# A hybrid streaming layer on one core: the sample tile's attention beside the last two tiles, in other slots, and two changes of timing in the scheduler

## The chip, the cores and the metric

The kernel runs on one core of one Trainium2 chip. The metric is device time in microseconds of the whole kernel; lower is better. A core has five engines that run side by side: TensorE (PE in the profile, with its weight loads as PEld), VectorE (DVE), ScalarE (ACT), GpSimd (POOL) and SyncE (SP), which issues most DMA transfers. Products go from PE into banks of PSUM, and ACT or DVE empty these.

## The reference

One encoder layer on 17 tiles of 128 frames: 16 tiles are one prompt of 2048 frames, and the last is the sample tile (8 running streams with 16 new frames each). Two mixers run on the same projection of the frames:

```python
p = jnp.einsum('btd,de->bte', x, w_in)      # q, k, v, gate of retention; q, k, v of attention
# retention, 4 heads of 128, by chunks, with a state s carried along
scores = jnp.einsum('bnhd,bmhd->bhnm', q, k) * dmask
o = jnp.einsum('bhnm,bmhe->bnhe', scores, v) + jnp.einsum('bnhd,bhde->bnhe', q, s) * q_decay
s_new = g * s + jnp.einsum('bmhd,bmhe->bhde', k * k_decay, v)
# banded attention, 8 query heads of 64 on 2 key heads: a chunk of 64 frames reads itself and two chunks before
p = sink_softmax(einsum(q, k_band) * 64 ** -0.5, sinks)      # one learned sink in the denominator
o = einsum(p, v_band)
# then
x = layer_norm(ALPHA * x + mix @ w_out);  y = layer_norm(ALPHA * x + relu(x @ w_up) ** 2 @ w_down)
```

For the sample tile each of the eight streams has its own cached window of 128 keys and values (`cache_swa_k`, `cache_swa_v`) beside its 16 new ones, and its own retention state (`state_ret`), of which the new one is an output.

## The kernel before, in words

**Tiles and groups.** The 17 tiles go in three groups: prompt tiles 0 to 4, tiles 5 to 10, and the sample tile (number 16) with tiles 11 to 15. In the third group the sample tile has index 0. Each group runs through the stages `kv`, `qk` (or `sq`), `ret`, `out`, `mlp`; tile names in the profile carry group and stage, so `sw_2ret` is a bank taken in stage `ret` of the third group (counted from 0). Single-precision operands are split into a rounded high part and the rest, and each product is three matmuls (`mm3`). In the second and third group, many products are made by a scheme of seven products in place of eight, for which sums and differences of operand blocks are needed: of weights (made once, kept in DRAM as `kept`, `keptd`, `keptq`, `keptv`) and of frames (`sums_task`, which makes T1 to T4 in the `xT` slots).

**Memory slots.** On-chip memory is cut into slots by tag: 14 `xT`, 10 `w`, 4 `raw`, 20 rows `y` of 512 numbers, 8 `u3` of 768, and in PSUM 2 banks `mm`, 2 `rt` and 4 `sw`. `take` takes a slot, `drop` gives it back, `room(tag, n)` asks whether n are free. `S.fence[name]` is the time, by the scheduler's own reckoning, when the last user of a slot is through with it.

**The scheduler.** The order of the instructions on each engine is fixed when the kernel is built, by a small scheduler (`Sched`). The main thread of the program issues the large products one after another; everything else is written as tasks (generators) that `yield` the time at which they want to go on. Before each three matmuls the main thread calls `S.pump()`, which lets the tasks run whose time has come by the scheduler's cost model. A `yield` thus puts off the issue of an instruction; what an engine does on the chip is then in that order. `S.ready(t, eng)` gives the reckoned time when t is written.

**What the change touches.**

- `sums_task` (stage `kv` and `qk`) makes T2 and T1, and when these are through, T3 and T4 in `xT` slots. In the third group, T1 and T2 are first stored to DRAM (`keptt`) since they are read again later. Its helper `put` copies the high part on ACT (L297), and makes the rest on DVE (L313).
- `vg_operands` makes 32 block sums of the gate and value weights during the MLP of the second group, each on a DVE and ACT pass, and stores them as `keptv`. `due` spaces them.
- `swa_task` goes through the attention of the five prompt tiles of the third group, in the order of indices 3, 4, 5, 1, 2. For the scores of a tile it takes all four `sw` banks; its softmax runs on DVE (row maximum, L337) and ACT (exponentials, L293).
- `swa_sample_task` does the sample tile's attention in two halves of four streams. It loads cached keys and values, makes scores (PE, 64x144), exponentials, transposes and value products. Before the change it starts when `swa_task` has ended (`after[3]`), and its buffers are `u3` slots.
- `pair_task` does retention for one tile and two heads. For the sample tile, it loads the old states of each head (`sold`), masks the values by stream (`vm`), makes the outputs, and in two `sw` banks the new states (`kvs`).
- `vg_units` is the main thread in stage `ret` of the third group: seven products times three pairs of tiles of the gate and value projection. Its `post` tasks empty the banks and start the retention of a tile when its parts are there.
- `units` is the order of the output projection, as pairs of half and tile index. In the loop over it, the next unit is staged (`stage_mix`, which waits until retention and attention of that tile are issued) before the products of the present one are issued:

```python
S.until(lambda: u in mts and all((h, units[ui + 1][1]) in ret_tasks for h in range(RH)))
stage_mix(units[ui + 1])
```

Of the kernel before, what the change touches and what calls it, by code (L numbers as in the profile page):

```python
# [14 lines left out]
P = 128  # L15
# [38 lines left out]
VGT = (2,)  # L54
# [125 lines left out]
def tile_layer(ctx: ExitStack, tc: tile.TileContext, A: dict, O: dict):  # L180
# [17 lines left out]
    def room(tag, n=1):  # L198
        return live[tag] + n <= CAP[tag]
# [5 lines left out]
    def take(tag, shape, dt=F32):  # L205
        if not room(tag):
            assert not S.inside, f"no room in {tag}"
            S.until(lambda: room(tag))
        live[tag] += 1
        cnt[0] += 1  # L210
        t = (psp if tag in PS else sb).tile(shape, dt, tag=tag, bufs=CAP[tag], name=f"{tag}_{ph[0]}_{cnt[0]}")
        name = t.tensor.name if hasattr(t, "tensor") else t.name
        tag_of[name] = tag
        S.fence[name] = min(freed[tag])
        freed[tag].remove(S.fence[name])
        return t
# [32 lines left out]
    def wait_room(tag, n=1):  # L249
        while not room(tag, n):  # L250
            yield S.now + 0.3
# [456 lines left out]
    def vg_operands():  # L708

        while at_pair[0] < 1.0 or ph[0] != "1mlp":  # L710
            yield S.now + 1.0
        stored = []

        def save(kt, i, o, hl):
            yield S.ready(hl, eng="SP") - 0.3
            dma(kept_v[o][kt].rearrange("p (x c) -> p x c", x=2)[:, :, 256 * i:256 * i + 256],
                hl.bitcast(F32).rearrange("p (x c) -> p x c", x=2))
            drop(hl)

        due = 0.0  # L720
        for n_ in range(8):
            kt, i = n_ // 2, n_ % 2
            while not room("y", 3):
                yield S.now + 0.3
            src = [take("y", [P, 2, 256]) for _ in range(2)]
            for x in range(4):
                g_ = 4 * (x % 2) + kt
                o = 512 * (g_ % 2) + 256
                dma(src[x // 2][:, x % 2, :], A["wret"][2 * (x // 2) + i, g_ // 2][:, o:o + 256])
            yield S.ready(*src) + 1.5  # L730
            a11, a12, a21, a22 = [src[x // 2][:, x % 2, :] for x in range(4)]
            for o, t, args in (("S1", a22, (a21, a22, ALU.add)), ("S3", a21, (a11, a21, ALU.subtract)),
                               ("S2", a11, (a22, a11, ALU.subtract)), ("S4", a12, (a12, a11, ALU.subtract))):
                while not room("y") or S.now < due:
                    yield S.now + 0.3
                due = S.now + 6.0
                hl = take("y", [P, 512], F32R)
                yield max(S.ready(*src, eng="DVE"), S.fence[hl.tensor.name])
                yield from idle("DVE", QUIET)
                vtt(t, *args)  # L740
                yield S.ready(t, eng="ACT")
                acopy(hl[:, 0:256], t)
                yield S.ready(hl[:, 0:256], eng="DVE")
                vtt(hl[:, 256:512], t, hl[:, 0:256].bitcast(F32), ALU.subtract)
                stored.append(S.add(save(kt, i, o, hl)))
            drop(*src)
        while not all(t[3] for t in stored):
            yield S.now + 0.3
        made_v.extend(kept_v)
# [360 lines left out]
    def sums_task(gi, T, used):  # L1110


        parts = []
        while (gi, "kv", 1) not in pieces:
            yield S.now + 0.3
        for i in range(2):
            while not room("u3", 4):
                yield S.now + 0.3
            parts.append([take("u3", [P, 2, 384]) for _ in range(4)])
            for t, (b, kk) in zip(parts[i], ((0, 0), (1, 0), (1, 1), (0, 1))):  # L1120
                dma(t, x_source(gi, b, 2 * kk + i))

        def put(o, t, i, slack):
            h, l = (x[:, 2 * i:2 * i + 2, :] for x in T[o])
            yield S.ready(t, eng="ACT")
            acopy(h, t)
            yield S.ready(h, eng="DVE")
            yield from idle(slack=slack)
            vtt(l, t, h.bitcast(F32), ALU.subtract)
            used[o] = i + 1  # L1130
            drop(t)

        def home(o):
            while not room("xT", 2):
                yield S.now + 0.3
            T[o] = (take("xT", [P, 4, 384], F32R), take("xT", [P, 4, 384], F32R))

        yield from home("T2")
        for x11, x12, x22, x21 in parts:
            yield S.ready(x11, x12, x22, x21, eng="DVE")  # L1140
            yield from idle(slack=XSLACK)
            vtt(x11, x12, x11, ALU.subtract)
            vtt(x12, x22, x12, ALU.subtract)
            vtt(x22, x22, x11, ALU.subtract)
            vtt(x21, x21, x22, ALU.subtract)
        for n_, o in ((2, "T2"), (0, "T1")):
            if o == "T1":
                yield from home(o)
            for i in range(2):
                yield from put(o, parts[i][n_], i, XSLACK)  # L1150
            if gi in VGT:
                stores[gi, o] = S.add(store_sum(o, T[o], list(norms)))
        for n_, o, before in ((1, "T3", "T2"), (3, "T4", "T1")):
            while used.get(before) != "over":
                yield S.now + 0.3
            yield from home(o)
            for i in range(2):
                yield from put(o, parts[i][n_], i, SLACK)
        if gi in VGT:
            return  # L1160
        while used.get("T3") != "over":
            yield S.now + 0.3
        while not room("xT", 2):
            yield S.now + 0.3
        xagain[gi, 1, 0] = 0
        h, l = xblocks[gi, 1, 0] = (take("xT", [P, 4, 384], F32R), take("xT", [P, 4, 384], F32R))
        for p in range(2):
            yield from wait_room("u3")
            r = take("u3", [P, 2, 384])
            dma(r, x_source(gi, 1, p))  # L1170
            yield S.ready(r, eng="ACT")
            split(h[:, 2 * p:2 * p + 2, :], l[:, 2 * p:2 * p + 2, :], r)
            drop(r)
            xagain[gi, 1, 0] = 2 * p + 2
# [273 lines left out]


    def swa_sample_task(ti, si, sq_tasks, qTs, kTall, vall, mix, after):  # L1450
        while not sq_tasks[ti] or not sq_tasks[ti][3] or not after[3]:
            yield S.now + 0.5
        qT = qTs[ti]
        for hb in range(2):
            yield from wait_room("u3", 5)
            kt, cv, vn = take("u3", [P, 4, 144]), take("u3", [P, 4, P]), take("u3", [32, 4, P])
            dma(kt[:, :, 0:128], A["ck"][4 * hb:4 * hb + 4].rearrange("b p k -> p b k"))
            dma(cv, A["cv"][4 * hb:4 * hb + 4].rearrange("b k f -> k b f"))
            ks = si * P + 64 * hb
# [4 lines left out]
                b = 4 * hb + i  # L1464
                dma(vn[0:16, i, :], vall[16 * b:16 * b + 16, si, :])
            yield S.soon(kt, cv, vn, qT)
            while not (room("sw", 2) and room("u3", 2)):
                yield S.now + 0.3
            ps, p = [take("sw", [P, 2, 144]) for pr in range(2)], [take("u3", [P, 2, 160]) for pr in range(2)]
            for i in range(4):  # L1470
                b = 4 * hb + i
                for g in range(2):
# [20 lines left out]
            for pr in range(2):  # L1493
                yield S.soon(p[pr])
                yield from wait_room("sw")
                pt = take("sw", [P, 4, P])
                for i in range(2):
                    transpose(pt[:, i, :], p[pr][:, i, 0:128])
                    transpose(pt[0:32, 2 + i, :], p[pr][:, i, 128:160])
                drop(p[pr])  # L1500
                yield from wait_room("u3")
                pts.append(take("u3", [P, 4, P]))
                acopy(pts[pr][:, 0:2, :], pt[:, 0:2, :])
                vcopy(pts[pr][0:32, 2:4, :], pt[0:32, 2:4, :])
                drop(pt)
# [15 lines left out]
                    b = 4 * hb + i  # L1521
                    copy(mix[gs, :, 16 * b:16 * b + 16], ov[gs, i, :].rearrange("p (j t) -> p j t", j=4))
            drop(ov)
            drop(kt, cv, vn)
        dropq[0](qT)
        swa_done.add(ti)

# [121 lines left out]
    def pair_task(t, h0, ps, qTs_, kTs_, done_qk, mix, made=None):  # L1649
# [41 lines left out]
        if smp:  # L1691
            for g, h in enumerate(hs2):
                op, k = bk[:, 2 + g, :], ks[g]
                while not (room("u3", 4) and room("sw", 2)):
                    yield S.now + 0.3
                hs = [slice(64 * hb, 64 * hb + 64) for hb in range(2)]
                sold = [take("u3", [P, 4, P]) for hb in range(2)]
                qp, vm = take("u3", [P, 2, 320]), take("u3", [P, 4, P])
                for hb in range(2):
                    dma(sold[hb], A["st"][h][:, 4 * hb:4 * hb + 4, :])  # L1700
                gzero(qp)
# [351 lines left out]
    for gi, tiles in enumerate(GROUPS):  # L2053
# [306 lines left out]
            rope = take("xT", [P, 6, P])  # L2360
            dma(rope[:, 0:n, :], A["rope"][goff:goff + n].rearrange("t p c -> p t c"))
        ret_tasks = {}
        units = [(0, ti) for ti in ((0, 3, 4, 5, 1, 2) if gi == 1 else (1,2,0,3,4,5) if gi in VGT else (0, 1, 2, 4, 3, 5))[:n]] + [(1, ti) for ti in ((4, 0, 2, 1, 3) if n == 5 else (0, 1, 2, 4, 3, 5))]

        keep = ("y", "y", "u3", "y", "u3") if n == 5 else None
        boxes, mts, xrs = {}, {}, {}
# [616 lines left out]
```

## Time and profile before

| | us |
|---|---|
| median of 3 runs | 2249.87 (2247.48 to 2254.01) |
| the profiled execution | 2248.2 |
| its span, first to last instruction | 2246.4 |
| PE busy in the span | 2223.6 |
| DVE / ACT busy | 1636.1 / 1021.0 |
| mean granted clock of TensorE | 0.997 |

Busy times of engines overlap. Matmuls are pipelined, so a busy PE is not PE at its peak. Rows of the profile show the line of a helper (L278 is every matmul, L284 every transpose, L297 every ACT copy, L313 every DVE tensor-tensor), so the tile names tell the steps apart. In rows of the timeline come start, duration, engine, line, operation, out<-in, shapes and count, and in brackets the idle time ahead of the row with what ended it. In rows of stretches come start and end, length, the busy time (and instructions) of PE, PEld, DVE, ACT and POOL, the granted clock as a share of full speed, the busy share of the DMA engines and GB/s. In rows of waits come who waited for whom, the total, how often, and the longest.

### The profile page before, as it was taken

Reading aid. Unit: us, or ns where it says so; the run is one execution under the profiler, and the core shown is the slowest. Engines: PE = TensorE matmul, PEld = TensorE weight load, DVE = VectorE, ACT = ScalarE, POOL = GpSimd, SP = SyncE. Lnnn points to the kernel's source line nnn. Section 1 sums busy time; section 2 is a strip of 40 time slices with the busy share of each in tenths; the row PEclk is TensorE's granted clock in tenths of the full one; section 3 lists DMA queues with packets and bytes.
Section 4 is the critical chain, followed back from the end, with each engine's and each line's share of the span. In section 5 each row is a group of like instructions: output and inputs, shape, how many; then the busy total and the mean of one; then the engine's idle time right before and its main releaser. Section 6 shows DMA issues by size and latency. Waiting matters only on the chain. (4 is left out here: it accounts for less than half of the span.)

```text
span 2246.4 us, 34610 instructions
## 1 busy us (share of the span) xinstructions
PE 2223.6 (99%) x12149; PEld 1971.3 (88%) x12149; DVE 1636.1 (73%) x3564; ACT 1021.0 (45%) x2407; POOL 96.3 (4%) x131
## 2 busy tenths in 40 slices
PE   9999999999999999999999999999999999999998
PEld 7788889999999988789999899899778999999987
DVE  6767689787877577787788877796775955555557
ACT  5534645555545555473344443366343732222222
POOL 0000000000000000000000000000010000000002
PEclk9999999999999999999999999999999999999999
DMA  7646758999989836767899998999555577777776
GB/s 262 212 169 212 282 196 306 322 328 336 319 320 349 282 127 221 265 242 249 289 345 341 342 324 289 333 344 348 208 185 191 171 256 252 248 259 255 251 255 182
DMA packets 228830, 598.91 MB, mean 267 GB/s; under 512 B 23216, under 2 KB 80304, under 8 KB 228656
## 3 DMA queue, kind: packets, MB, share of 16 engines
q1 hardware_dynamic: 223472, 587.26, 74.5%
q0 software_dynamic: 5184, 9.44, 2.5%
q8 instruction: 96, 1.57, 0.3%
q14 instruction: 78, 0.64, 0.1%
HBM read 401.25 MB, written 185.86 MB: 261 GB/s over the span
## 5 line engine op out<-in xcount | busy, mean ns | idle before, releaser
L278 PE MATMUL sw_1mlp<-xT_1out,w_1mlp 128*128 128x384 f32 x1152 | 209.5, 336 | 0.2 <-DMA w_1mlp<-kept 0.2
L278 PE MATMUL sw_2mlp<-xT_2out,w_2mlp 128*128 128x384 f32 x1152 | 209.0, 336 | 0.3 <-DVE kvln_2mlp L313 0.3
L278 PEld LDWEIGHTS sw_1mlp<-xT_1out,w_1mlp 128*128 128x128 f32 x1152 | 202.0, 188 | 4.9 <-DMA w_1mlp<-kept 1.2
L278 PEld LDWEIGHTS sw_2mlp<-xT_2out,w_2mlp 128*128 128x128 f32 x1152 | 202.1, 188 | 4.3 <-DVE kvln_2mlp L313 0.6
L278 PE MATMUL sw_0mlp<-xT_0out,w_0mlp 128*128 128x320 f32 x1188 | 179.1, 309 | 0.0
L278 PEld LDWEIGHTS sw_0mlp<-xT_0out,w_0mlp 128*128 128x128 f32 x1188 | 176.5, 188 | 2.2
L278 PE MATMUL rt_2mlp<-w_2mlp,u_2mlp 128*128 128x512 f32 (+1 forms) x522 | 127.1, 388 | 0.0
L278 PE MATMUL rt_1mlp<-w_1mlp,u_1mlp 128*128 128x512 f32 x516 | 126.8, 391 | 0.0
L278 PE MATMUL rt_0mlp<-w_0mlp,u_0mlp 128*128 128x512 f32 x492 | 121.1, 391 | 1.5 <-DVE u_0mlp L313 1.4
L278 PE MATMUL mm_2mlp<-w_2mlp,u_2mlp 128*128 128x512 f32 (+1 forms) x504 | 122.5, 388 | 0.0
L278 PE MATMUL mm_1mlp<-w_1mlp,u_1mlp 128*128 128x512 f32 x492 | 121.3, 391 | 0.0
L278 PEld LDWEIGHTS rt_2mlp<-w_2mlp,u_2mlp 128*128 128x128 f32 x522 | 96.9, 188 | 19.0
L278 PEld LDWEIGHTS rt_1mlp<-w_1mlp,u_1mlp 128*128 128x128 f32 x516 | 96.5, 188 | 19.2
L278 PE MATMUL mm_0mlp<-w_0mlp,u_0mlp 128*128 128x512 f32 x456 | 112.2, 393 | 0.0
L278 PEld LDWEIGHTS rt_0mlp<-w_0mlp,u_0mlp 128*128 128x128 f32 x492 | 92.0, 188 | 20.7 <-DVE u_0mlp L313 1.9
L278 PEld LDWEIGHTS mm_2mlp<-w_2mlp,u_2mlp 128*128 128x128 f32 x504 | 93.6, 188 | 18.4
L278 PEld LDWEIGHTS mm_1mlp<-w_1mlp,u_1mlp 128*128 128x128 f32 x492 | 92.0, 188 | 18.3
L278 PEld LDWEIGHTS mm_0mlp<-w_0mlp,u_0mlp 128*128 128x128 f32 x456 | 85.9, 190 | 17.3
L313 DVE TENSOR_TENSOR w_1mlp<-w_1mlp,w_1mlp 128x512 fp32r<-128x512 f32 x120 | 81.7, 687 | 12.7 <-ACT w_1mlp L297 11.6
L313 DVE TENSOR_TENSOR w_0mlp<-raw_0mlp,w_0mlp 128x512 fp32r<-128x512 f32 (+1 forms) x69 | 63.5, 922 | 34.7 <-ACT w_0mlp L297 18.8
L297 ACT CAST u_2mlp<-kvln_2mlp 128x384 fp32r<-128x384 f32 x51 | 26.2, 515 | 117.7 <-PE mm_2mlp L278 44.1
L297 ACT CAST w_1mlp<-w_1mlp 128x512 fp32r<-128x512 f32 x84 | 52.0, 619 | 57.7 <-PE sw_1mlp L278 49.0
(1019 smaller groups left out, 4813.4 us busy)
## 6 DMA issues: line engine op xcount, KB each, us to landing
w_1mlp<-kept SPq DMA_DIRECT2D x104, 512.0 KB, 5.5
w_2mlp<-kept SPq DMA_DIRECT2D x104, 512.0 KB, 4.0
w_2mlp<-keptd SPq DMA_DIRECT2D x98, 512.0 KB, 4.2
kept<-w_0mlp SPq DMA_DIRECT2D x96, 512.0 KB, 5.0
keptd<-w_1mlp SPq DMA_DIRECT2D x84, 512.0 KB, 4.5
keptq<-y_0mlp SPq DMA_DIRECT2D x72, 256.0 KB, 5.1
w_1qk<-keptq SPq DMA_DIRECT2D x34, 512.0 KB, 5.9
w_2qk<-keptq SPq DMA_DIRECT2D x34, 512.0 KB, 6.9
```

Source lines behind the costliest of these rows:

```text
L278: S.run("PE", lambda: nc.tensor.matmul(out, lhsT, rhs, start=start, stop=stop, skip_group_check=again), [out], [lhsT, rhs], cost)
L297: S.run("ACT", lambda: nc.scalar.copy(out, in_), [out], [in_], 0.06 + 0.83e-3 * size(out))
L313: S.run("DVE", lambda: nc.vector.tensor_tensor(out, a, b, op), [out], [a, b], dcost(out))
```

## The change

Five edits:

1. `vg_operands`: the sums are spaced by 8.0 in place of 6.0.
2. `put` in `sums_task` yields until the slot that it writes is free by the scheduler's reckoning, and not only until its source is there.
3. `swa_sample_task` starts when three tiles' attention is done. Per half, if an `xT` slot and six rows are free, it takes its keys and values in one `xT` slot (`wide`) and the rest in rows `y`; else it takes `u3` slots as before.
4. `pair_task` for the sample tile takes the old states and masked values in rows `y` if five are free.
5. `units` of the third group begins with indices 1, 0, 2 in place of 1, 2, 0.

```diff
@@ vg_operands
-                due = S.now + 6.0
+                due = S.now + 8.0
@@ sums_task, put
-            yield S.ready(t, eng="ACT")
+            yield max(S.ready(t, eng="ACT"), *[S.fence[x.tensor.name] for x in T[o]])
@@ swa_sample_task
-        while not sq_tasks[ti] or not sq_tasks[ti][3] or not after[3]:
+        while not sq_tasks[ti] or not sq_tasks[ti][3] or len(swa_done) < 3:
...
-            yield from wait_room("u3", 5)
-            kt, cv, vn = take("u3", [P, 4, 144]), take("u3", [P, 4, P]), take("u3", [32, 4, P])
+            while not room("u3", 5) and not (room("xT") and room("y", 6)):
+                yield S.now + 0.3
+            tag = "y" if room("xT") and room("y", 6) else "u3"
+            vn = take(tag, [32, 4, P])
+            if tag == "y":
+                wide = take("xT", [P, 1088])
+                kt, cv = wide[:, 0:576].rearrange("p (b k) -> p b k", b=4), wide[:, 576:1088].rearrange("p (b k) -> p b k", b=4)
+            else:
+                kt, cv = take("u3", [P, 4, 144]), take("u3", [P, 4, P])
...
-            while not (room("sw", 2) and room("u3", 2)):
+            while not (room("sw", 2) and room(tag, 2)):
...
-            ps, p = [take("sw", [P, 2, 144]) for pr in range(2)], [take("u3", [P, 2, 160]) for pr in range(2)]
+            ps, p = [take("sw", [P, 2, 144]) for pr in range(2)], [take(tag, [P, 2, 160]) for pr in range(2)]
...
-                yield from wait_room("u3")
-                pts.append(take("u3", [P, 4, P]))
+                yield from wait_room(tag)
+                pts.append(take(tag, [P, 4, P]))
...
-            drop(kt, cv, vn)
+            drop(vn, *([wide] if tag == "y" else [kt, cv]))
@@ pair_task, sample tile
-                while not (room("u3", 4) and room("sw", 2)):
+                while not (room("sw", 2) and (room("u3", 4) or (room("u3") and room("y", 5)))):
...
-                sold = [take("u3", [P, 4, P]) for hb in range(2)]
-                qp, vm = take("u3", [P, 2, 320]), take("u3", [P, 4, P])
+                tag = "y" if room("y", 5) else "u3"
+                sold = [take(tag, [P, 4, P]) for hb in range(2)]
+                qp, vm = take("u3", [P, 2, 320]), take(tag, [P, 4, P])
@@ units
-        units = [... (1,2,0,3,4,5) if gi in VGT ...
+        units = [... (1,0,2,3,4,5) if gi in VGT ...
```

More of the change, by code (lines that the diff above doesn't have):

```diff
@@ L2362, in tile_layer @@
         ret_tasks = {}
-        units = [(0, ti) for ti in ((0, 3, 4, 5, 1, 2) if gi == 1 else (1,2,0,3,4,5) if gi in VGT else (0, 1, 2, 4, 3, 5))[:n]] + [(1, ti) for ti in ((4, 0, 2, 1, 3) if n == 5 else (0, 1, 2, 4, 3, 5))]
+        units = [(0, ti) for ti in ((0, 3, 4, 5, 1, 2) if gi == 1 else (1,0,2,3,4,5) if gi in VGT else (0, 1, 2, 4, 3, 5))[:n]] + [(1, ti) for ti in ((4, 0, 2, 1, 3) if n == 5 else (0, 1, 2, 4, 3, 5))]
         keep = ("y", "y", "u3", "y", "u3") if n == 5 else None
```

## The prediction

> **What bounds the kernel now.** I read the page's first part, then stretches of the stage that the change touches, then what TensorE (PE) waited for in it.
>
> ```profile
> span 2246.4 us, 34610 instructions
> PE 2223.6 (99%) x12149; PEld 1971.3 (88%) x12149; DVE 1636.1 (73%) x3564; ACT 1021.0 (45%) x2407; POOL 96.3 (4%) x131
> ```
>
> The profiled execution took 2248.2 us: this span and 1.8 us around it. It lies 1.7 us under the median of the three runs, 2249.87 (2247.48 to 2254.01). PE is idle for 2246.4 - 2223.6 = 22.8 us in all, so no edit that leaves its work as it is can win much more than 1%. This change leaves every product in place, so I look for the idle time it can reach. The stretches below are the third group's gate and value products with three of its attention tiles (1569.2 to 1628.5), the same with the last two tiles (to 1669), with the sample tile (to 1686.5), the first output unit with the sample tile's rest (to 1702.9), and output units alone.
>
> ```profile
> core 0: us, PE busy (x) PEld busy (x) DVE busy (x) ACT busy (x) POOL busy (x), PEclk, DMA share, GB/s
> 1569.20:1628.50 59.30, 56.67 (x347) 42.87 (x345) 44.60 (x130) 22.18 (x77) 3.35 (x5) 0.97 0.60 211
> 1628.50:1669.00 40.50, 40.33 (x282) 31.04 (x278) 30.43 (x96) 17.87 (x66) 3.91 (x8) 1.00 0.58 195
> 1669.00:1686.50 17.50, 17.50 (x143) 15.22 (x142) 14.10 (x56) 8.26 (x33) 2.64 (x4) 1.00 0.43 149
> 1686.50:1702.90 16.40, 15.52 (x135) 13.10 (x133) 12.88 (x51) 7.28 (x26) 1.60 (x4) 1.00 0.49 174
> 1702.90:1740.80 37.90, 37.90 (x172) 31.13 (x169) 19.72 (x41) 12.04 (x27) 1.62 (x2) 1.00 0.59 205
> ```
>
> PE's idle time here is 2.63, 0.17, 0, 0.88 and 0 us: 3.7 us where the change works. PE's waits from 1566 to 1703 name it:
>
> ```profile
> PE sw_2ret L278 <- ACT u_2ret L293: 2.3, 1, 2.3
> PE rt_2out L278 <- ACT xT_2ret L293: 0.6, 1, 0.6
> PE rt_2ret L278 <- ACT y_2ret L293: 0.3, 1, 0.3
> PE rt_2ret L278 <- ACT xT_2ret L293: 0.3, 1, 0.3
> ```
>
> The long one stands in the timeline of PE at 1609.2, and the clock row by row shows that it costs more than its gap:
>
> ```profile
> 1608.14 1.09 PE L278 MATMUL rt_2ret<-u_2ret,u_2ret 128*64 128x128 f32 x16
> 1611.51 2.47 PE L278 MATMUL sw_2ret<-u_2ret,y_2ret 64*128 64x512 f32 x4 [2.27 <-ACT u_2ret L293]
> 1609.20:1611.50 2.30, 0.04 (x2) 0.00 (x0) 0.61 (x3) 1.58 (x7) 0.00 (x0) 1.00 0.68 218
> 1612.50:1613.50 1.00, 1.00 (x3) 0.10 (x1) 0.69 (x1) 1.00 (x7) 0.00 (x0) 0.63 0.00 0
> 1613.50:1614.50 1.00, 1.00 (x4) 0.59 (x3) 0.48 (x1) 0.55 (x4) 0.00 (x0) 0.50 0.27 104
> 1614.50:1615.50 1.00, 1.00 (x6) 1.00 (x6) 0.20 (x1) 0.00 (x0) 0.00 (x0) 0.50 0.42 158
> 1615.50:1616.50 1.00, 1.00 (x8) 1.00 (x7) 0.00 (x0) 0.00 (x0) 0.00 (x0) 0.67 0.70 262
> ```
>
> The clock lost there is 0.37 + 0.50 + 0.50 + 0.33 = 1.7 us of full-speed work, so this one wait is worth 2.3 + 1.7 = 4.0 us. [...]
>
> **The frame sums ask for their slot first (the max with S.fence in put).** At present the ACT copy is issued while its slot is still being stored to DRAM, and what stands behind it on ACT and DVE waits too:
>
> ```profile
> 1528.71 0.83 ACT L297 CAST xT_2qk<-u_2kv 128x768 fp32r<-128x768 f32 x1 [11.57 <-DMA keptt_T<-xT_2kv]
> 1530.66 0.96 DVE L313 TENSOR_TENSOR xT_2qk<-u_2kv,xT_2qk 128x768 fp32r<-128x768 f32 x1 [9.56 <-DMA keptt_T<-xT_2kv]
> 1529.97 4.43 PE L278 MATMUL mm_2qk<-xT_1mlp,w_2qk 128*128 128x384 f32 x24 [0.91 <-ACT y_2qk L297]
> 1534.29 1.83 DVE L313 TENSOR_TENSOR xT_2qk<-u_2kv,xT_2qk 128x768 fp32r<-128x768 f32 x2 [1.13 <-DMA keptt_T<-xT_2qk]
> 1542.56 2.76 PE L278 MATMUL rt_2qk<-xT_2qk,w_2qk 128*128 128x384 f32 x15
> ```
>
> ACT stood for 11.57 us with copies that empty PSUM queued behind it, and PE ran out of a bank for 0.91 us. The new wait is in the kernel's own scheduler, not on the engine, so the PSUM copies pass. I take -0.9. What is late next is the sum itself: its splits end at 1536.1 now and its first reader on PE starts at 1542.56, 6.4 us of cover. Without that cover each later us would be PE's. Bounds: -0.9 if the wait goes, and +0.6 (the largest of the short waits above) if the splits come late instead. The wait is the row itself, so I stay at that end.
>
> **Weight sums spaced wider (6.0 to 8.0).** These are the 32 block sums of the gate and value weights, made in the second group's MLP.
>
> ```profile
> L359 SPq DMA_DIRECT2D keptv_S<-y_1mlp x32: 524/525/1396, 1095.6 to 1321.8; - x32
> L359 SPq DMA_DIRECT2D w_2qk<-keptv_S x1: 332/332/332, 1567.4 to 1567.4; - x1
> 1096.00:1322.00 226.00, 225.82 (x1140) 204.64 (x1139) 183.23 (x342) 101.93 (x211) 0.00 (x0) 1.00 0.97 341
> ```
>
> 32 stores in 226.2 us are 7.3 us apart. With 2 us more for each of 31 steps the last would fall 62 us later, at 1384; with 8.0 us as the whole step it falls at 1344. The first reader is at 1567.4, so at least 183 us cover it. Two source rows and one result row are held up to 62 us longer. The DMA engines are at 0.97 of their time there and get a little easier, but PE is idle for only 0.18 us of that stretch: 0, with bounds -0.2 and +0.6 (again a short wait, should the longer hold of rows stop something).
>
> **The sample tile's retention in rows.** The old states and the masked values move from u3 slots to y rows when five rows are free. Its loads, memset, copies and products are the same in number, so it issues nothing more on SP or POOL. It asks for two sw banks as before; and the long wait above is just that: the state product (sw out of u3 and y) sits in a bank that a softmax of the third attention tile still reads on ACT. A place in y does not free that bank. I take 0. Bounds: -4.0 if the small shifts ahead of it put the two in another order, and +4.0 if they make a second such wait; 0 is nearest to the row, since the code that chose the bank is untouched.
>
> **The sample tile's attention after three tiles instead of after five.** Its place in PE's order now, with the output units behind it:
>
> ```profile
> 1626.85 1.68 PE L278 MATMUL rt_2ret<-u_2ret,kvln_2kv 128*64 128x256 f32 x16
> 1645.55 1.68 PE L278 MATMUL sw_2ret<-u_2ret,kvln_2kv 128*64 128x256 f32 x16
> 1665.62 1.68 PE L278 MATMUL sw_2ret<-u_2ret,kvln_2kv 128*64 128x256 f32 x16
> 1668.98 1.20 PE L278 MATMUL sw_2ret<-u_2ret,raw_2qk 64*64 64x144 f32 x16
> 1692.10 1.20 PE L278 MATMUL sw_2out<-u_2ret,raw_2qk 64*64 64x144 f32 x16
> 1701.71 1.30 PE L278 MATMUL sw_2out<-u_2out,u_2ret 128*64 128x64 f32 x32
> 1702.94 4.43 PE L278 MATMUL mm_2out<-w_2ret,u_2out 128*128 128x512 f32 x18
> 1686.50:1704.20 17.70, 3.53 (x56) 2.85 (x56) 1.56 (x4) 3.27 (x18) 1.00 0.45 162
> ```
>
> The first three rows are the value products of the third, fourth and fifth tile. The sample tile's scores follow the fifth at once, its second half at 1692.1, and its end at 1703.0; the second output unit starts on it. So the sample tile now spans 34.0 us. The last row, on the banks of the second half alone, prices a half: PE 3.53, DVE 1.56, ACT 3.27 us. All of that moves to after 1628.5, and none of it is removed. Moving 7.1 us of PE work out of a tail that holds 0.88 us of idle time wins at most 0.88. In the tail remain the retention tasks of the last tiles, whose chain through ACT and DVE made both waits there (0.6 and 0.3), now with 48 output products between them where 24 stood. Where the work goes, DVE has 30.43 of 40.5 us busy and gets at least 3.1 more (83%), ACT 17.87 and 6.5 (60%). That leaves both below full, but a short wait can come of it. The loads of cached keys and values go out earlier on SP; DMA is at 0.58 there. They hold one xT slot and three rows (six must be free at the start), which value products and thirds of retention also ask for. I take -0.9 for the tail and +0.4, the mean of the two waits at 0.6 and 0.3, for a new one: -0.5, with bounds -0.9 and +6 (below).
>
> **Output units in the order 1, 0, 2.** Same products. It makes the loop ask for the sample tile one unit sooner. 0 if that tile is done by 1686.5.
>
> **The sum.** 2248.2 - 0.9 + 0 + 0 - 0.5 = 2246.8 us; at the median's distance that would be 2248.5.
>
> **Rivals.**
> *The long wait goes too.* Everything ahead of 1609 shifts by the 0.9 us and by other slots; the state product needs to come only about 2.3 us later, or ahead of that tile's scores. For it: one coincidence of two tasks. Against it: the same check for the bank. 2246.8 - 4.0 = 2242.8. [...]
>
> *The sample tile comes too late (the slower one).* The loop stages the next unit before it issues the present one, so with the sample tile second, no output product leaves before that tile is done. Begun at 1628.5, its 34.0 us end at 1662.5, 24 us ahead of 1686.5. But each attention tile wants all four sw banks, and tiles come 18.7 and 20.1 us apart; if each half must wait for one such turn, that is 38.8 us, and the end is at 1701 again. Then 24 products (18 take 4.43, so 5.9 us) are lacking as filler, and gaps like the one at 1609 lose 1.7 us of clock: 2248.2 - 0.9 + 5.9 + 1.7 = 2254.9, or 2253.2 without the clock; 2254. It decides from an end later than 1686.5.
>
> *The change doesn't act:* rows and xT slot are not free at 1628.5, the task falls back to u3 or waits, and ACT still meets the unfinished store: 2248.2.
>
> *PE is not full.* Weight loads (PEld) are at 0.72, 0.77, 0.87 and 0.80 in the first four stretches against 0.821 among plain output units. At 0.821 all through, the 102.2 us of loads there would take 124.5 us in place of 133.7: 9.2 us less, 2248.2 - 9.2 - 0.9 = 2238.1. [...] Against it speaks the 1.68 us for the same 16 products in each of three places: small products are slow wherever they stand, and an order does not mend that.
>
> **How the numbers follow.** About 0.3% (6.7 us) is what a measurement of this kernel can tell from no change. Forecast 0.50 (own range 2244 to 2250); long wait gone 0.23; too late 0.14; no effect 0.08; PE not full 0.05. Faster by over 0.3% means below 2241.5: the last case and two fifths of the second, 0.05 + 0.09 = 0.14. Slower means above 2254.9: half of the late case and a little of the forecast for a second long wait, 0.07 + 0.03 = 0.10. The same: 0.76. The range goes down to 2240, past the 4.0 us, and up to 2254.
>
> **What would show it.** Right: no ACT wait of many us on keptt; no PE wait of mm_2qk on y_2qk; the last store from y_1mlp to keptv_S between 1344 and 1384; 64x144 scores soon after the third tile's value products and an end before 1686; the state product's wait on ACT near 1609 still there, with half clock behind it; less than 0.5 us idle between the last value product and the second output unit. Wrong: that wait gone, or a new PE wait above 1 us, first of all on the sample tile's result before the first output unit, or on a PSUM bank between 1628 and 1686.

## The result, and the profile after

| | before | after |
|---|---|---|
| median, same chip | 2249.87 us (2245.65 to 2254.01, 9 runs) | 2243.05 us (2240.72 to 2244.95, 9 runs) |
| ratio | | 0.9973, 95% interval 0.9963 to 0.9983 |
| profiled execution, its span | 2248.2, 2246.4 | 2241.8, 2240.0 |

The change wins 0.27%, about 6 us by the ratio; the medians differ by 6.8. The time lies in the predicted range, but 3.8 us under the forecast of 2246.8 and outside that forecast's own range (2244 to 2250). It is nearest to the rival "the long wait goes too" (2242.8), to which I gave a chance of 0.23. Both of these count from the profiled 2248.2: as a change, 1.4 us less was forecast and 5.4 less by that rival, and the profiled executions differ by 6.4.

The first row of after's page, and what PE waited for from the start of stage `qk` to the end of the output projection:

```profile
PE 2221.1 (99%) x12149; PEld 1969.8 (88%) x12149; DVE 1636.8 (73%) x3564; ACT 1021.9 (46%) x2407; POOL 95.8 (4%) x131
```

```profile
PE rt_2ret L278 <- DMA y_2ret<-in_st_dram: 0.6, 2, 0.5
PE rt_2ret L278 <- ACT xT_2ret L293: 0.3, 1, 0.3
PE sw_2ret L284 <- ACT u_2ret L293: 0.3, 1, 0.3
PE sw_2ret L278 <- DMA u_2ret<-in_ck_dram: 0.2, 1, 0.2
```

PE is idle for 2240.0 - 2221.1 = 18.9 us in all, where it was 22.8. The wait of 2.3 us is gone, that of `mm_2qk` too (before, it stood at 1529.97 with 0.91). What is left is short. The first, third and last row are new, and the first and last are waits for loads: of old retention states (`in_st`) and of cached keys (`in_ck`).

To see where the time came from I cut both traces at the first PE row of a stage; these are the rows of after, and the first products of `qk`, `ret` and `mlp` are where the cuts are:

```profile
1476.09 1.73 PE L278 MATMUL sw_2qk<-xT_1mlp,w_1mlp 128*128 128x384 f32 x9
1565.58 1.78 PE L278 MATMUL mm_2ret<-w_2qk,xT_1mlp 128*128 128x512 f32 x7
1760.87 0.60 PE L284 MATMUL sw_2mlp<-cst,y_2out 128*128 128x128 f32 x4
```

And of before:

```profile
1478.57 1.21 PE L278 MATMUL sw_2qk<-xT_1mlp,w_1mlp 128*128 128x384 f32 x6
1569.25 1.08 PE L278 MATMUL mm_2ret<-w_2qk,xT_1mlp 128*128 128x512 f32 x4
1767.58 0.60 PE L284 MATMUL sw_2mlp<-cst,y_2out 128*128 128x128 f32 x4
```

| stretch | before | after | difference |
|---|---|---|---|
| up to `qk` of the third group | 1478.57 | 1476.09 | -2.48 |
| `qk` | 90.68 | 89.49 | -1.19 |
| `ret` and output projection | 198.33 | 195.29 | -3.04 |
| the rest | 478.83 | 479.13 | +0.30 |

The first line is not shown to come from the change: PE has hardly a gap where the sums are made (0.04 us of 248, below), and in the profiled executions of the two kernels and the experiments that start lies anywhere from 1474.8 to 1480.2, with and without each edit. The two stretches in the middle hold 4.2 us of the 6.4 us between these two executions; that the time came so close to the rival's 2242.8 is in part luck, since 2.5 us stand in that first line.

In `qk`, the rows of PE and ACT of after at the place of the old wait, and the last split with its first reader:

```profile
1526.41 4.32 PE L278 MATMUL mm_2qk<-xT_1mlp,w_2qk 128*128 128x384 f32 x24
1526.61 0.48 ACT L297 COPY y_2qk<-sw_2qk 128x384 f32<-128x384 f32 x1 [1.60 <-PE sw_2qk L278]
1527.12 1.57 ACT L297 CAST xT_2qk<-u_2kv 128x768 fp32r<-128x768 f32 x2
1535.91 0.96 DVE L313 TENSOR_TENSOR xT_2qk<-u_2kv,xT_2qk 128x768 fp32r<-128x768 f32 x1 [0.16 <-ACT xT_2qk L297]
1538.89 4.32 PE L278 MATMUL rt_2qk<-xT_2qk,w_2qk 128*128 128x384 f32 x24
```

ACT's copies out of PSUM now pass ahead of the copy into the slot and wait there for nothing but PE; `mm_2qk` has no bracket. The price shows in the last two rows: the splits end at 1536.87, and the first product that reads them starts 2.0 us later, where there were 6.4 us.

In `ret`, the same banks before and after. Of before:

```profile
1601.12 1.13 PE L278 MATMUL sw_2ret<-u_2ret,y_2ret 64*128 64x512 f32 x4
1602.18 1.68 PE L278 MATMUL sw_2ret<-u_2ret,kvln_2kv 128*64 128x256 f32 x16
1604.91 1.57 PE L278 MATMUL sw_2ret<-kvln_2kv,raw_2qk 64*128 64x192 f32 x16
```

Of after:

```profile
1595.99 1.68 PE L278 MATMUL sw_2ret<-u_2ret,kvln_2kv 128*64 128x256 f32 x16
1599.04 1.13 PE L278 MATMUL sw_2ret<-y_2ret,y_2ret 64*128 64x512 f32 x4
1601.69 1.57 PE L278 MATMUL sw_2ret<-kvln_2kv,raw_2qk 64*128 64x192 f32 x16
1612.22 1.13 PE L278 MATMUL sw_2ret<-y_2ret,y_2ret 64*128 64x512 f32 x4
```

The 64x512 rows are the new states of the sample tile's heads, the 128x256 rows the second attention tile's values, the 64x192 rows the third tile's scores. Before, the order was head 0, values, scores, and PE came to head 1 at 1609.2, 4.3 us after the scores began, and waited 2.3 us until that tile's softmax left the bank. After, the values come first, then head 0, then the scores, and head 1 follows 10.5 us after them, at 1612.22; the softmax is over by then (its last row on ACT ends at 1609.54). Counted from the start of `ret`, the values come 2.5 us earlier than before, head 0 1.6 us later, the scores 0.5 us later, and head 1 6.7 us later than PE came to it before. A coincidence of two tasks is undone, though no edit says anything about their order.

The sample tile's attention of after (first half, second half, last products), and the tail:

```profile
1627.27 1.20 PE L278 MATMUL sw_2ret<-u_2ret,raw_2qk 64*64 64x144 f32 x16 [0.19 <-DMA u_2ret<-in_ck_dram]
1645.34 1.20 PE L278 MATMUL sw_2ret<-xT_2ret,raw_2qk 64*64 64x144 f32 x16
1662.31 0.68 PE L278 MATMUL sw_2ret<-y_2ret,y_2ret 32*64 32x64 f32 x16
```

```profile
1625.00:1664.00 39.00, 37.73 (x313) 28.61 (x312) 31.27 (x107) 19.41 (x90) 3.87 (x8) 1.00 0.58 186
1686.18:1702.90 16.72, 16.72 (x97) 14.40 (x96) 13.30 (x48) 5.70 (x15) 2.08 (x4) 1.00 0.52 174
```

It ends at 1663.0, 23 us ahead of the first output product. Only its second half is in the new slots; the first still took `u3`. The tail has lost its 0.88 us of idle time, but the stretch with the sample tile now holds 1.27 us.

### The profile page after: what moved, and what is told of

It is laid out like the page before. It is cut to its first block, busy times and chain, and to the rows that moved or that the text cites. A ratio compares the mean times of both kernels' runs of the same rounds, so it can differ in the third digit from the quotient of the medians.

```text
span 2240.0 us, 34600 instructions
## 1 busy us (share of the span) xinstructions
PE 2221.1 (99%) x12149; PEld 1969.8 (88%) x12149; DVE 1636.8 (73%) x3564; ACT 1021.9 (46%) x2407; POOL 95.8 (4%) x131
## 5 line engine op out<-in xcount | busy, mean ns | idle before, releaser
L313 DVE TENSOR_TENSOR w_1mlp<-w_1mlp,w_1mlp 128x512 fp32r<-128x512 f32 (+1 forms) x120 | 81.7, 686 | 14.9 <-ACT w_1mlp L297 14.0
L313 DVE TENSOR_TENSOR w_0mlp<-raw_0mlp,w_0mlp 128x512 fp32r<-128x512 f32 (+1 forms) x69 | 63.5, 921 | 34.8 <-ACT w_0mlp L297 18.9
```

The source lines that it names most:

```text
L313: S.run("DVE", lambda: nc.vector.tensor_tensor(out, a, b, op), [out], [a, b], dcost(out))
```

## The experiments

Theory A: edit 2 carries the gain, by the `qk` wait directly and by the order of states, values and scores in `ret`. Edit 3 pays nothing by itself. Theory B: moving the sample tile's attention carries it. Theory C: the retention rows (edit 4) moved the state product.

The kernels ran in three sessions, each beside the kernel before, whose medians there were 2247.9, 2249.93 and 2248.61 us. "Qk" and "ret, out" are the two middle stretches of the profiled execution, cut as above; "clock" is the granted clock of the whole span, averaged over the timed runs. The ratios are as recorded; they are not quotients of the medians and differ from those by up to 0.05%.

| label | edits | median us | ratio, 95% interval | qk | ret, out | head 1 waits | clock |
|---|---|---|---|---|---|---|---|
| (before, profiled) | none | | | 90.68 | 198.33 | 2.3 | 0.9977 (33 runs) |
| no_slot_first | 1, 3, 4, 5 | 2246.22 | 0.9995, 0.9986 to 1.0004 | 90.84 | 196.38 | 2.3 | 0.9975 |
| no_slot_first_later_head | the same, head 1 later | 2243.59 | 0.9983, 0.9974 to 0.9992 | 90.31 | 194.77 | none | 0.9985 |
| no_retention_rows | 1, 2, 3, 5 | 2242.55 | 0.9977, 0.9968 to 0.9986 | 89.50 | 197.20 | none | 0.9988 |
| spacing_alone | 1 | 2246.24 | 0.9994, 0.9985 to 1.0003 | 93.31 | 199.21 | 2.3 | 0.9978 |
| changed_again | all | 2242.55 | 0.9970, 0.9958 to 0.9982 | 89.50 | 196.15 | none | 0.9987 |
| two_edits | 2, 3 | 2244.60 | 0.9977, 0.9966 to 0.9988 | 89.49 | 196.12 | none | 0.9986 |
| attention_and_order | 3, 5 | 2251.42 | 1.0009, 0.9998 to 1.0019 | 90.97 | 201.04 | 2.3 | 0.9973 |
| early_loads | all, loads earlier | 2240.39 | 0.9957, 0.9941 to 0.9973 | 89.49 | 194.40 | none | 0.9988 |
| changed_beside_early | all | 2242.51 | 0.9976, 0.9967 to 0.9984 | 89.50 | 195.24 | none | 0.9987 |
| early_loads_again | all, loads earlier | 2240.26 | 0.9968, 0.9956 to 0.9980 | 89.49 | 193.75 | none | 0.9986 |
| attention_later_head | 3, head 1 later | 2244.84 | 0.9984, 0.9976 to 0.9993 | 91.16 | 194.37 | none | 0.9985 |

**Without edit 2.** The changed kernel, with the old line in `put`:

```diff
-            yield max(S.ready(t, eng="ACT"), *[S.fence[x.tensor.name] for x in T[o]])
+            yield S.ready(t, eng="ACT")
```

> The changed kernel without its second edit (put asks for its source alone again, as before); the four other edits stay. Theory A, that the second edit carries the gain, by itself (0.9 us on PE in qk) and by shifting the sample tile's retention against the third attention tile (4.0 us): ACT waits over 10 us on keptt again, PE waits about 2.3 us near 1609 with half clock behind it, and the time is that of the kernel before, 2248 to 2251 us. Theory B, that the sample tile's attention beside the last two tiles carries it: 2243 to 2246 us.

The gain is gone: the interval of the ratio holds 1. The median is 1.8 us under theory A's 2248 to 2251, in a session in which the kernel before was 2.0 us lower than in the first measurement. The profile has all three old waits, on ACT, in `qk` and at head 1, though four of the five edits are in; the half clock that I expected behind the last one did not come (1.00 from 1610 to 1618, see the last section).

```profile
1526.59 0.83 ACT L297 CAST xT_2qk<-u_2kv 128x768 fp32r<-128x768 f32 x1 [11.74 <-DMA keptt_T<-xT_2kv]
1527.85 4.43 PE L278 MATMUL mm_2qk<-xT_1mlp,w_2qk 128*128 128x384 f32 x24 [1.08 <-ACT y_2qk L297]
1609.41 1.93 PE L278 MATMUL sw_2ret<-y_2ret,y_2ret 64*128 64x512 f32 x4 [2.27 <-ACT u_2ret L293]
```

The last row reads `y_2ret`: the old states lie in rows, and the wait is there all the same. So edit 4 does not take it away.

**The same, with head 1 later.** In `pair_task`, ahead of the second wait for banks:

```diff
                 yield S.soon(qp, vm, *sold)
+                if h == 1:
+                    yield S.now + 5.0
                 while not room("sw", 2):
```

> As the run without the second edit, and the sample tile's retention of head 1 puts off its last products by 5.0 us in the scheduler, so that the state product does not meet the banks of the third tile's softmax. It prices the long wait alone. Theory A: the wait near 1609 and its half clock go, the 11 us of ACT on keptt and 0.9 us of PE in qk stay: 3.5 to 4.5 us under the run without the second edit, about 2245. Theory B has the gain elsewhere: no change against that run beyond 1.5 us.

Head 1 then follows the scores by 10.0 us and does not wait (the row of its products stands at 1613.58 without a bracket). The median falls by 2.6 us against the kernel without these two lines: more than theory B's 1.5, less than the 3.5 to 4.5 of theory A. The `qk` wait is still there (0.5 us in this execution).

**Without edit 4.** The `pair_task` hunk of the diff undone.

> The changed kernel without its fourth edit: the sample tile's old states and masked values lie in u3 slots again. Theory A: the time of the changed kernel, 2242 to 2244 us; the two waits of PE on the loads of old states (0.6 us together in the changed kernel) may go. Theory C, that the other slots moved the state product away from the busy bank: the wait of 2.3 us near 1609 is back, about 2247.

The time of the changed kernel, and no wait at head 1: theory C falls for the state product. Its profile has two load waits, 1.8 and 1.2 us on `in_ck`, so its 197.20 is the longest stretch without the old wait; its profiled execution was also the slowest of its 11 runs (2247.80), so I read nothing further from it.

**Edit 1 alone.** `due = S.now + 8.0`, nothing else.

> The kernel before with the first edit alone (block sums of gate and value weights spaced by 8.0). Theory A: the last store moves from 1322 to 1344 to 1384 and nothing else, the time of before within 1 us. Theory D, that the DMA engines at 0.97 in that stretch cost something: 1 us or more faster.

No gain that can be told: the ratio stands for 1.3 us less, which would be theory D's side of 1 us, but the interval reaches from 3.4 us less to 0.7 us more. The last store is at 1355.3, as theory A has it. Its profile is of use for another reason: the two waits of before fell worse in it.

```profile
PE sw_2ret L278 <- ACT u_2ret L293: 2.3, 1, 2.3
PE mm_2qk L278 <- ACT y_2qk L297: 2.0, 1, 2.0
```

```profile
1530.00:1534.00 4.00, 4.00 (x16) 4.00 (x15) 2.17 (x3) 3.92 (x8) 0.00 (x0) 0.57 1.00 396
1612.00:1620.00 8.00, 7.46 (x22) 5.28 (x23) 2.99 (x12) 3.09 (x17) 0.46 (x1) 0.57 0.18 68
```

Behind the `qk` wait of 2.0 us the clock stood at 0.57 over 4 us, which is 1.7 us lost (4 x 0.43). Behind the wait at head 1 it stood at 0.57 over 8 us: 3.4 us lost.

**The changed kernel again**, and beside the kernels of the third session:

> The changed kernel as it is, beside the others on the same chip. All theories: 2242 to 2244.5, a ratio of 0.996 to 0.998 to the kernel before. Its profile shows again no wait on keptt, no wait of mm_2qk on y_2qk and no wait above 1 us of the sample tile's retention between 1600 and 1615.

> The changed kernel as it is, on the chip of the two others: 2241 to 2244.5, ratio 0.996 to 0.998 to the kernel before.

Both as expected: with the first measurement, ratios of 0.9973, 0.9970 and 0.9976, and `qk` 89.49 or 89.50 in each profile.

**Edits 2 and 3 alone.** Edit 2 was not measured by itself: with the old start of the sample tile's attention, the scheduler's tasks would wait for each other. So edit 3 goes with it, and what is said of edit 2 here holds with edit 3 in the kernel.

> Only edits 2 and 3: the frame sums ask for their slot, and the sample tile's attention starts after three tiles. Spacing, retention slots and unit order are as before. Theory A (edit 2 carries the gain, and needs edit 3 only so that the tasks don't wait for each other): the time of the changed kernel within 1.5 us, 2241.5 to 2245; no keptt wait, no mm_2qk wait, no 2.3 us wait on u_2ret. Theory C (retention in rows, or the order of the units, carries part of it): 1.5 to 4 us above the changed kernel.

A win of 0.23%, with the `qk` stretch of the changed kernel and the new order in `ret` (values 1599.11, head 0 1602.15, scores 1604.81, head 1 1615.58, no wait). Its median is 2.1 us above the changed kernel's, outside the 1.5 us of theory A and inside the range of theory C. But the intervals of the ratios overlap over most of their length, and the two stretches agree (196.12 against 196.15). So whether edits 1, 4 and 5 together give something is open.

**Edits 3 and 5.**

> Only edits 3 and 5: the sample tile's attention after three tiles, and the unit order; the frame sums don't ask for their slot. Theory A: the time of the kernel before within 1.5 us (ratio 0.9990 to 1.0006), with the keptt wait of 11 to 12 us on ACT, a wait of mm_2qk of 0.5 to 2 us and the 2.3 us wait on u_2ret all there, although the tail from 1686 to 1703 has no wait left. Theory B (moving the sample tile's attention pays by itself): 2243 to 2245, ratio 0.997 to 0.998. My prediction took -0.5 us for this edit.

Theory B falls: no gain, if anything a loss (the ratio of 1.0009 is a little above theory A's 1.0006 too). Its rows:

```profile
1603.70 1.57 PE L278 MATMUL sw_2ret<-kvln_2kv,raw_2qk 64*128 64x192 f32 x16
1610.30 2.58 PE L278 MATMUL sw_2ret<-u_2ret,y_2ret 64*128 64x512 f32 x4 [2.27 <-ACT u_2ret L293]
1665.38 0.69 PE L278 MATMUL sw_2ret<-y_2ret,xT_2ret 128*64 128x64 f32 x16 [0.88 <-ACT u_2ret L293]
```

```profile
1611.00:1619.00 8.00, 8.00 (x25) 5.78 (x25) 4.50 (x18) 1.84 (x11) 0.69 (x1) 0.57 0.25 84
1690.70:1707.00 16.30, 16.30 (x99) 14.04 (x99) 11.17 (x39) 5.46 (x15) 1.38 (x2) 1.00 0.64 220
```

The tail behind its last gate and value product has no idle time, as the edit promises, and the sample tile waits 0.88 us at 1665 instead: as much idle time has come back in another place. The rest is the old wait at head 1, here with 3.4 us of clock behind it.

**Edit 3 with head 1 later.** Edit 3 and the two lines above.

> Only edit 3, and the second head of the sample tile's retention asks for its banks 5.0 later by the scheduler's reckoning, so that the third tile's softmax is over by then. The frame sums don't ask for their slot, so the keptt wait on ACT and the qk wait of 0.5 to 2 us on PE stay. If the long wait with its clock is worth 2.7 us (as the two kernels without edit 2 gave) or 4.0 us (as I worked out from one execution): 2245.5 to 2247.5, ratio 0.9980 to 0.9990. If the wait at that place costs nothing by itself: ratio 0.9995 to 1.0010, as for edits 3 and 5 alone. If it and not the qk wait carries all of the gain: 0.9970.

A ratio of 0.9984 where edits 3 and 5 without the two lines gave 1.0009, with the `qk` wait still there (1.4 us). The stretch `ret, out` is 194.37 against 201.04. So the wait at head 1 carries more than half of the gain by these ratios (0.16% of 0.24% to 0.30%); the interval, 0.07% to 0.24%, also allows less. The ratio is inside the forecast for a wait worth 2.7 to 4.0 us, the median 0.7 us under it.

**Loads earlier.** In the changed kernel the sample tile's loads stand on SP's DMA queue among those of the weight sums. The keys of its first half (`u_2ret`) go out behind three that took 2.2 us, those of its second half (`xT_2ret`) behind three more that took 10 us:

```profile
1618.49 2.19 SPq L359 DMA_DIRECT2D w_2ret<-keptv_S x3
1620.78 0.38 SPq L359 DMA_DIRECT2D u_2ret<-in_ck_dram x1
1624.62 10.07 SPq L359 DMA_DIRECT2D w_2ret<-keptv_S x3
1634.75 0.90 SPq L359 DMA_DIRECT2D y_2ret<-in_st_dram x2
1635.74 0.85 SPq L359 DMA_DIRECT2D w_2ret<-halves_out x2
1636.65 1.08 SPq L359 DMA_DIRECT2D xT_2ret<-in_ck_dram x1
```

The experiment takes slots and issues loads once two tiles are through, and lets only the scores wait for three:

```diff
-        while not sq_tasks[ti] or not sq_tasks[ti][3] or len(swa_done) < 3:
+        while not sq_tasks[ti] or not sq_tasks[ti][3] or len(swa_done) < 2:
...
                 dma(vn[0:16, i, :], vall[16 * b:16 * b + 16, si, :])
+            while len(swa_done) < 3:
+                yield S.now + 0.5
             yield S.soon(kt, cv, vn, qT)
```

> The changed kernel, but the sample tile's attention takes its slots and issues its loads once two tiles are through, while its scores still wait for three. It is meant to get the loads of cached keys ahead of those of the weight sums in SP's queue. If the short waits on in_ck and in_st (0.2 and 0.6 us) are all that the changed kernel loses there: 0 to 0.8 us less than the changed kernel, which cannot be told from it. If holding an xT slot and six rows longer stops a retention task: a new PE wait of 1 us or more, and 1 to 4 us more.

> The changed kernel with the sample tile's slots taken and its loads issued after two tiles, scores after three. If its 2.2 us below the changed kernel in the last session came from the load waits (in_ck 1.2 us and in_st 0.4 us there): 1 to 2.5 us below the changed kernel again. If it was only how the executions fell: within 0.8 us of it.

The first half's keys are now asked for 29 to 30 us earlier than in the changed kernel (1590.22 against 1619.48 beside it and 1620.78 above):

```profile
1590.22 0.67 SPq L359 DMA_DIRECT2D u_2ret<-in_ck_dram x1
1637.76 0.61 SPq L359 DMA_DIRECT2D xT_2ret<-in_ck_dram x1
```

PE's wait on the first half's keys (0.2, 1.2 and 0.2 us in the three profiles of the changed kernel) is gone. The second half's keys come no earlier, as the last row shows, so the 10 us in the queue are not what this experiment takes away.

Both times the median lies 2.2 us under the changed kernel's of the same session, and each of the 11 runs (2239.09 to 2242.49) is under that kernel's median (2242.55 and 2242.51). This is the fastest version measured, and faster than the kernel before by 0.32% to 0.43%; against the changed kernel the intervals overlap, so the difference is likely and not certain. The first forecast (0 to 0.8 us less) was too small, the second (1 to 2.5) was met. But the profiles do not show where 2.2 us would come from. `ret, out` is shorter by 0.8 to 2.4 us, and the rest is longer by 0.6 to 0.9, part of which may be only where the first product of `mlp` falls among the output products. PE's idle time in `ret, out` is 1.7 and 1.1 us against 1.8, 2.8 and 2.0 in the changed kernel, 0.8 us less on average. And the two profiled executions, each the slowest of its kernel's runs, took 2242.30 and 2242.49 us, no less than the changed kernel's in the same sessions (2241.41 and 2242.44). The cause is open beyond that 0.8 us.

## Why the prediction was right or wrong

**The step that failed** is edit 4's term, "I take 0", with the statement that the state product's wait stays. The argument was that the code that chose the bank is untouched. That is true, and it does not follow that the order is. The order is fixed by the times at which tasks wake, and edit 2, 80 us earlier, moved them. Of the profiles, all seven with edit 2 have head 1 without a wait, and the four without it that leave head 1 alone have 2.3 us there. I had seen the way it could go ("small shifts ahead of it put the two in another order") and gave it too little weight; and it hangs on edit 2, not on edit 4: the kernel without edit 4 has the new order, the one without edit 2 the old. By which task the earlier wake-up reached the states was not followed.

**What that wait is worth.** I worked out 4.0 us from one execution (2.3 idle, 1.7 of clock). The runs bear out the size as a mean: adding the two lines moved the ratio by 0.12% (2.7 us) in one pair of one session, and by 0.25% (5.6 us) in the other, of two sessions and with edit 5 out besides. The four profiles with the wait have 196.38 to 201.04 us in `ret, out`, mean 198.7; the three of the changed kernel 195.24 to 196.15, mean 195.6: 3.2 us. Against the two kernels that put head 1 later without edit 2 (194.77 and 194.37) it is 4.2 us; the changed kernel's stretch is 1.0 us longer than theirs, and has the loads as its new waits.

**Edit 2, -0.9.** The sign and the mechanism were right: no ACT wait on `keptt`, no wait of `mm_2qk`. The size was too small, because one execution gave it. The wait was 0.5, 0.9, 1.1, 1.2, 1.4 and 2.0 us in the six profiles without edit 2, and in the last one clock was lost too. The `qk` stretch has 90.31 to 93.31 us there, mean 91.2, against 89.49 or 89.50 in all seven with edit 2: 1.7 us, and a stage that no longer varies. "What is late next" was named rightly and did no harm: 2.0 us of the 6.4 us of cover are left.

**Both together:** 1.7 + 3.2 = 4.9 us of the 5.4 to 6.7 us that the three ratios of the changed kernel give. The remaining us or so is within their intervals and has no cause shown.

**Edit 1, 0:** no change clear of the noise (0.9985 to 1.0003), and the last store where it was forecast between 1344 and 1384. The group of DMA issues of after, and PE's stretch under it (247.96 of 248.00 us busy):

```profile
L359 SPq DMA_DIRECT2D keptv_S<-y_1mlp x32: 524/525/1492, 1093.7 to 1354.4; - x32
```

```profile
1096.00:1344.00 248.00, 247.96 (x1255) 225.58 (x1254) 200.41 (x372) 110.27 (x226) 0.00 (x0) 1.00 0.95 333
```

**Edit 3, -0.5:** the tail gave its 0.88 us, and the new short waits took them back (1.27 us idle between 1625 and 1664, +0.4 was forecast). I had these come through ACT and DVE; they came mostly through SP's queue (0.8 us on `in_st` and `in_ck`), which the prediction named only by saying that the loads "go out earlier on SP", and did not price. The larger part, 0.6 us on `in_st`, is the old states of retention: the two kernels with edit 2 and without edit 4 do not have it, and wait longer on `in_ck` instead (1.8 and 1.2 us in `no_retention_rows`, 1.0 and 0.6 us in `two_edits`). With edit 5 it measured +0.1% (-0.02% to +0.19%) where -0.02% was forecast; edit 5 by itself was not measured.

**The rivals.** "Too late" falls: the forecast end was 1662.5 without a turn lost, and it came at 1663.0, 23 us ahead of the first output product. That the two agree so closely is luck: the tile took 35.7 us and not 34.0, and `ret` began 3.7 us earlier. "Doesn't act" was true of half a tile: the first half fell back to `u3`, and nothing hung on that. "PE is not full" falls: 16 value products take 1.68 us as before.

## What to carry to other kernels

A copy into a slot that a transfer is still reading stopped every copy queued behind it on its engine, here for 11.2 to 12.6 us in the six profiles without edit 2; make the scheduler wait for the slot, and let the copies that empty PSUM pass. Before calling a wait untouched by an edit, ask whether its order is written down or falls out of wake-up times upstream; if it falls out, give "it goes" and "it stays" both a real chance. And take the price of a wait from several executions, since a stage's length over many of them tells more than one bracket.

## What the runs showed of the hardware

The same wait of 2.26 or 2.27 us at head 1 cost no clock in one profiled execution, 1.7 us in another and 3.4 in two. No loss, without edit 2:

```profile
1607.10:1609.40 2.30, 0.04 (x2) 0.00 (x0) 0.61 (x2) 1.59 (x7) 0.00 (x0) 1.00 0.62 216
1612.00:1614.00 2.00, 2.00 (x14) 1.79 (x14) 1.15 (x9) 0.00 (x0) 0.00 (x0) 1.00 0.70 262
```

So in these profiles a gap of about 2 us (these four, and the one of 2.0 us in `qk`) was a draw, and the amounts drawn were 0, 1.7 and 3.4 us; waits of 1.4 us and less in `qk` cost no clock (1.00 in each microsecond from 1476 to 1567 in the five profiles that have them), nor did one of 1.75 us in `no_retention_rows` (the twelve 128x512 products soon behind it took 3.03 us, 0.25 us each, where six in the stretch at 0.57 of `spacing_alone` took 2.25 us, 0.38 us each). What decides the amount is not shown.

The loss also shows in the timed runs: the kernels with the wait at head 1 have a mean clock of 0.9973 to 0.9978, those without it 0.9985 to 0.9988. In the kernel without edit 2 the two lines that put head 1 later raised it from 0.9975 to 0.9985, and 0.0010 of the span is 2.2 us of full-speed work, close to the mean of the four draws, 2.1 us. With the 2.3 us of the gap itself that makes the wait about 4.4 us on average, an estimate. Whether the runs also spread less without it is not shown: in the first measurement the 9 runs of the changed kernel span 4.2 us and the 9 of before 8.4, but in the experiments (5 to 12 runs each) the kernels with the wait span 5.9 to 7.1 us and those without it 3.2 to 8.4.
